# Two gate pairs by seven products instead of one, 18 filler blocks instead of 20, and tiles of their own for the scan's x, in a hybrid attention and state-space block

## The chip, the cores and the metric

The kernel runs on one core of a Trainium2 chip. The metric is the device time of one execution in microseconds (us). Five engines work side by side and wait for one another by semaphores: PE (TensorE, matmuls), ACT (ScalarE), DVE (VectorE), POOL (GpSimd) and SP (SyncE), which here does nothing but issue DMA transfers, in the order of its queue.

## The reference, cut to what matters

One layer: a token mixer of three branches (multi-head latent attention, forgetting attention, Mamba-2 scan), each gated by a sigmoid, then a gated MLP. S = 1024 positions, width 1024.

```
hn = rms_norm(x, norm_mix_g)
u_mla, u_fox, u_ssm, u_gate = split(hn @ w_in)
y_a = mla_branch(u_mla) @ w_br_mla;  y_b = fox_branch(u_fox) @ w_br_fox
y_c = ssm_branch(u_ssm) @ w_br_ssm
g = sigmoid(u_gate + b_gate)                  # 3 x 1024 columns
x = x + (g0*y_a + g1*y_b + g2*y_c) @ w_out
x = x + conv_ffn(rms_norm(x, norm_ffn_g))

ssm_branch: z, xBC, dt = split(u_ssm); xBC = silu(causal_dwconv(xBC))
            xs, B, C = split(xBC); y = ssd_scan(xs*dt, ...) + xs*D
            return rms_norm(y * silu(z))
ssd_scan:   by chunks: y = (C B^T * decay) x  +  C h * exp(a);  h = h*decay + B^T (decay x)
```

The gates need 3 x 1024 columns of `hn @ w_in`: 24 blocks of 128 columns, called gate blocks here. Their only reader is the product with the branches, late in the kernel.

## The kernel before, in words

Each fp32 operand of a matmul is split into a high and a low part (`..h`, `..l`), and three products are made (high x high, high x low, low x high). The high part is an ACT copy (L134), the low part a DVE subtraction (L135, and L1400 for filler weights). A matmul is 128x128 by 128x512.

The kernel goes through stages. Times are from the start of the profiled span: projections and their norms (to 396 us), the **convolution phase** (396 to 541), the **attention** of 16 heads (541 to 877), the **scan** in 8 chunks of 128 positions (877 to 1079), the branch products with the gates (L2145), the output product, and the MLP.

**Convolution phase.** It works in units n = 0, 1, ... A unit makes two blocks of 128 columns at once with seven half-size products (`c_product`, 12 matmuls each, L1224: 84 matmuls) where two blocks made directly take 96. Units 0 to 5 make the 12 blocks of xBC, whose convolution (`conv`) is stored to `xbc_d` (L1238); each unit from 6 on makes one pair of gate blocks (`pair_gates`), stored to `g_d` (L1309). `GP` is the number of these pairs. For a unit the sums of weights are made on POOL (`conv_sums`) and split on ACT and DVE. At the end one more gate block, `gates[1]`, is made directly (L1321, 48 matmuls); its weights are `raw_b` (L1261).

**Filler.** The other gate blocks (`all_fill`, 48 matmuls each, L1428, tiles `mm`) are put between the matmuls of the attention and the scan, so that PE has work while these wait for other engines. A block's weights are loaded (`wr`, L1392), split (`wh`, `wl`), and its result passes through ACT's tanh to a tile of the ring `f_t4` (four tiles, tag `t4`) and to `g_d` (L1438). In the attention a planner, the class `Sim`, writes out the order of PE, ACT, DVE and POOL; its second argument is the microseconds of filler by its own costs that it may spread over the heads (10.4 for a block). What is left is `f_left`; `FILL_SSD` gives an eighth of (`f_left` - 29) to each step of the scan.

**Scan.** Chunk c goes through three generators: `ssd_a` (loads; the transposes of x, L1922, tiles `stp` of a ring of two PSUM banks; B's transposes and C B^T in a third use of that ring, L1933 and L1935; on DVE `xd` L1941, `xddl` L135, `bTl`, and `cbm` L1938, which reads the bank of L1935), `ssd_b` (state update L1964 and its DVE part, `hsl`) and `ssd_c` (outputs `py` L1990, norm, transposes of y). `merge` interleaves `ssd_a` of chunk c, `ssd_b` of c-1, `ssd_c` of c-2 and filler on PE by fixed costs; the other engines follow a scheduler's order. Since the ring `stp` has two banks, the first group of x transposes of chunk c+1 takes the bank that C B^T of chunk c stood in, and cannot start before `cbm` of chunk c has read it.

The x tile of a chunk (`load_xs`, L1908, from `xbc_d`) is taken from the ring `f_t4`, which the filler outputs and z tiles (L1969) use too; `ssd_a` of chunk c, after its own transposes of x, asks for that of chunk c+1.

Of the kernel before, what the change touches and what calls it, by code (L numbers as in the profile page):

```python
# [11 lines left out]
F32 = mybir.dt.float32  # L12
# [9 lines left out]
P = 128  # L22
D = 1024
S = 1024
NT = S // P
# [17 lines left out]
def block_kernel(ctx: ExitStack, tc: tile.TileContext, x, positions, norm_mix_g, w_in, b_gate,  # L43
# [7 lines left out]
    def TP(name, bufs, **kw):  # L51
        if kw.get("space") != DRAM:
            kw["reuse_waits"] = "tile"
        return tc.tile_pool(name=name, bufs=bufs, **kw)
# [72 lines left out]
    def uid(s):  # L127
        cnt[0] += 1
        return f"{s}_{cnt[0]}"
# [495 lines left out]
    with ExitStack() as pm:  # L625
# [165 lines left out]
        def fx_bank():  # L791
            return acc("fx", "mv" if units % 3 == 2 else "mm")
# [179 lines left out]
            yield  # L972

    gates = [(b, j) for b in (1, 0, 2) for j in range(NK)]
    GP = 1

    def gate_cols(b, j):
        return w_inv[:, :, C_G + b * D + j * P:C_G + b * D + j * P + P]
# [57 lines left out]
    with ExitStack() as px:  # L1036
# [70 lines left out]
        for n, (which, c0) in enumerate(chunks):  # L1107
# [11 lines left out]
            for t in range(NT):  # L1119
# [8 lines left out]
                p = fx_head[t] if units < 6 else fx_bank()  # L1128
# [30 lines left out]
        for half in range(2):  # L1159
            p = fx_bank()  # L1160
# [30 lines left out]
    with ExitStack() as pc_:  # L1191
# [24 lines left out]
        def c_bank():  # L1216
            return psp.tile([P, 512], F32, name=uid("cb"), tag="up", bufs=6)
# [34 lines left out]
        late = []  # L1252
        last_n = 5 + GP
        for n in range(last_n + 1):
# [61 lines left out]
        for half in range(2):  # L1316
            p = c_bank()
# [64 lines left out]
    f_t4 = Ring(fpl, [P, S], F32, "t4", 4)  # L1382
# [27 lines left out]
    def all_fill():  # L1410

        blocks = [(b, j, C_G + b * D + j * P) for b, j in gates[2 + 2 * GP:]]
        f_left[0] = 10.4 * len(blocks)
# [33 lines left out]
    fill = all_fill()  # L1447
# [57 lines left out]
    def load_head(pool, br, h):  # L1505
        o = Head()
        o.br, o.h = br, h
        if (8 * br + h) % 2 == 0:
            t = [e[:, i, :] for e in (w0p.tile([P, 2, S], F32R, name=uid(n), tag=n) for n in ("w0h", "w0l"))
                 for i in range(2)]  # L1510
        else:
            t = [pool.tile([P, S], F32R, name=uid(n), tag=n, bufs=1) for n in ("qk0", "qk1", "qk2", "qk3")]
        if br == 0:
            parts = ((0, 0, k_h), (1, 0, k_l), (2, 0, q_h), (3, 0, q_l))
            kh, kl, qh, ql = (e[0:96] for e in t)
            o.passes = ((t[2][0:104], t[0][0:104]), (qh, kl), (ql, kh))
        else:
            parts = ((0, 0, fk_h), (1, 0, fk_h[:, 0:64, :]), (1, 64, fk_l), (2, 0, fq_h), (2, 64, fq_h), (3, 0, fq_l))
            o.passes = ((t[2], t[1]), (t[3][0:68], t[0][0:68]))
        for i, r, src in parts:  # L1520
            n = src.shape[1]
            SY.dma_start(f32(t[i][r:r + n, :]), src[h])
        return o

    def load_values(pool, o):
        o.vv = pool.tile([P, NT, P], F32R, name=uid("vv"), tag="vv")
        SY.dma_start(f32(o.vv), (v_d, fv_d)[o.br].rearrange("(t p) h c -> p t h c", p=P)[:, :, o.h, :])
# [174 lines left out]
    with ExitStack() as pt__:  # L1702
# [144 lines left out]
        with tc.manual_schedule(engines={mybir.EngineType.PE, mybir.EngineType.Activation, mybir.EngineType.DVE,  # L1847
                                         mybir.EngineType.Pool}):
            work = 227.0
            sm = Sim(fill, 86, work, 2.0)  # L1850
            sim[0] = sm
            ends = {}

            def head(hd, at):
                heads[hd] = load_head(atp, *names[hd])
                load_values(atp, heads[hd])
                loaded_at[hd] = at

            def make(hd):
                for jp in range(4):  # L1860
                    rows_, v = unit_tasks(sm, hd, jp, 4 * hd + jp)
                    ends[hd] = (rows_[-1].last, v)
                if hd + 2 < 16:
                    s_, v_ = ends[hd]
                    sm.add(Task("D", (0.3, 0.3), lambda hd=hd: head(hd + 2, sm.now.start + 8.0), [s_, v_], 0.0, (0, hd)))

            made = [0]

            def more(q=None):
                if made[0] < 16 and made[0] in heads:  # L1870
                    make(made[0])
                    made[0] += 1

            head(0, 1.0)
            head(1, 6.0)
            more()
            more()
            sm.run(more)
            clk[0] = max(sm.free.values())
            sim[0] = None  # L1880
# [8 lines left out]
    frp = pfr.enter_context(TP("frp", 1, side="right"))  # L1889
    with ExitStack() as ps__:  # L1890
# [12 lines left out]
            SY.dma_start(o.bc, xbc_d[8:12, :, c * P:c * P + P].rearrange("j p s -> p j s"))  # L1903

        def load_xs(o, c):
            o.xs, _ = f_t4.get()
            o.xs = o.xs.rearrange("p (j s) -> p j s", j=8)
            SY.dma_start(o.xs, xbc_d[0:8, :, c * P:c * P + P].rearrange("j p s -> p j s"))  # L1908

        def hb(t, c, hs=slice(0, 16)):  # L1910
# [2 lines left out]
        def ssd_a(o, c):  # L1913

            if c + 1 < NT:
                load_bc(obj[c + 1], c + 1)
                load_rows(obj[c + 1], c + 1)
            xT = pool.tile([P, D], F32, name=uid("xT"), tag="xT", bufs=1)
            for g in range(2):
                pt = psp.tile([P, 512], F32, name=uid("stp"), tag="tp", bufs=2)  # L1920
                for j in range(4):
                    T.transpose(pt[:, j * P:j * P + P], o.xs[:, 4 * g + j, :], ident)  # L1922
                A.activation(xT[:, 512 * g:512 * g + 512], pt, AF.Copy)
                yield 0.44
            yield 0.0
            if c + 1 < NT:
                load_xs(obj[c + 1], c + 1)
            o.bT = [pool.tile([P, 2, P], F32R, name=uid(n), tag=n) for n in ("bTh", "bTl")]
            o.c_ = [pool.tile([P, 2, P], F32R, name=uid(n), tag=n) for n in ("Ch", "Cl")]
            cbm = pool.tile([P, 2, P], F32, name=uid("cbm"), tag="cbm")  # L1930
            pt = psp.tile([P, 4, P], F32, name=uid("stp"), tag="tp", bufs=2)
            for g in range(2):
                T.transpose(pt[:, g, :], o.bc[:, g, :], ident)  # L1933
            for g in range(2):
                T.matmul(pt[:, 2 + g, :], o.bc[:, g, :], o.bc[:, 2 + g, :], start=True, stop=True)  # L1935
            split(*o.bT, pt[:, 0:2, :])
            split(*o.c_, o.bc[:, 2:4, :])
            V.tensor_mul(cbm, pt[:, 2:4, :], tri.unsqueeze(1).to_broadcast([P, 2, P]))  # L1938
            xv = xT.rearrange("p (h d) -> p h d", d=64)
            o.xd = pool.tile([P, 16, 64], F32, name=uid("xd"), tag="xd")  # L1940
            V.tensor_mul(o.xd, xv, hb(dt, c))  # L1941
            o.xdd = [pool.tile([P, 16, 64], F32R, name=uid(n), tag=n, bufs=1) for n in ("xddh", "xddl")]
            xdd = pool.tile([P, 16, 64], F32, name=uid("xdd"), tag="xdd", bufs=1)
            if c + 1 < NT:
                G.tensor_mul(xdd, xv, hb(dend, c))
            o.y = pool.tile([P, 16, 64], F32, name=uid("y"), tag="y", bufs=3)
            G.tensor_mul(o.y, xv, Db.unsqueeze(2).to_broadcast([P, 16, 64]))
            yield 0.65
            o.E = []
            for q in range(4):  # L1950
                E = pool.tile([P, 4, P], F32, name=uid("E"), tag="E", bufs=4)
                for hh in range(4):
                    h = 4 * q + hh
                    A.activation(E[:, hh, :], o.row[:, h, :], AF.Relu, scale=-1.0, bias=cumc[:, c, h:h + 1])
                A.activation(E, E, AF.Exp, scale=-1.0)
                V.tensor_mul(E, E, cbm[:, q // 2:q // 2 + 1, :].to_broadcast([P, 4, P]))
                o.E.append(E)
                if q == 1 and c + 1 < NT:
                    split(*o.xdd, xdd)
                yield 0.0  # L1960
# [71 lines left out]
        with tc.manual_schedule(engines={mybir.EngineType.PE}):  # L2032
            obj = {c: Head() for c in range(NT)}
            load_bc(obj[0], 0)
            load_xs(obj[0], 0)
            load_rows(obj[0], 0)
            merge([], 6.0)
            grain[0] = 4
            for c in range(NT + 2):
                st = []  # L2040
                if c < NT:
                    st.append((ssd_a(obj[c], c), 1.6))
                if 0 <= c - 2 < NT:
                    st.append((ssd_c(obj[c - 2], c - 2), *((0.88, 0.6) if c <= NT else (8.0, 0.2))))
                if 0 <= c - 1 < NT:
                    st.append((ssd_b(obj[c - 1], c - 1, obj.get(c - 2)), 6.4, 0.05))
                merge(st, FILL_SSD[c])
            for _ in range(4):
                if advance(fill) is None:
                    break  # L2050
# [234 lines left out]
    for t, nh in units:  # L2285
# [20 lines left out]
        p = head[t] if early else psp.tile([P, 512], F32, name=uid("wo"), tag="up", bufs=6)  # L2306
# [323 lines left out]
```

## Time and profile before

| | |
|---|---|
| median of three runs | 1989.72 us (1987.88, 1989.72, 1990.76) |
| profiled execution | 1986.64 us, its span 1984.9 us, mean granted clock 0.998 |
| convolution phase, in the span | 396.42 to 540.58 us |
| attention | 540.58 to 877.50 us |
| scan | 877.50 to 1079.15 us |
| matmuls of L1224 / L1321 / L1428 | 588 / 48 / 960 |

The profile lists how long each engine was busy; the chain of work that ended last, followed back from the end; and, for any stretch, busy times and single instructions with the idle time before them in square brackets and what released them. Matmul ends are modelled: matmuls that run back to back overlap in these records, so a matmul's price is the distance between starts. The 12 matmuls of a product or of a filler piece are grouped as x12 in the chain.

### The profile page before, as it was taken

Reading aid. Unit: us, or ns where it says so; the run is one execution under the profiler, and the core shown is the slowest. Engines: PE = TensorE matmul, PEld = TensorE weight load, DVE = VectorE, ACT = ScalarE, POOL = GpSimd, SP = SyncE. Lnnn points to the kernel's source line nnn. Section 1 sums busy time; section 2 is a strip of 40 time slices with the busy share of each in tenths; the row PEclk is TensorE's granted clock in tenths of the full one; section 3 lists DMA queues with packets and bytes.
Section 4 is the critical chain, followed back from the end, with each engine's and each line's share of the span. In section 5 each row is a group of like instructions: output and inputs, shape, how many; then the busy total and the mean of one; then the engine's idle time right before and its main releaser. Section 6 shows DMA issues by size and latency. Waiting matters only on the chain.

```text
span 1984.9 us, 28475 instructions
## 1 busy us (share of the span) xinstructions
PE 1958.7 (99%) x10101; PEld 1668.1 (84%) x10101; DVE 1397.4 (70%) x2156; ACT 965.8 (49%) x1678; POOL 701.3 (35%) x666
## 2 busy tenths in 40 slices
PE   9999999999999999998999999999999999999999
PEld 8989888888899988887888888888878888888887
DVE  7777567879566766757884575558997777766555
ACT  5555322355466666766774232225554444544432
POOL 5133232056123222213340351101664444423655
PEclk9999999999999999999999999999999999999999
DMA  6166856333645556545665785333323211249575
GB/s 180 53 197 212 269 189 211 103 106 112 197 123 145 134 144 149 145 127 172 179 193 172 260 289 190 124 121 107 106 85 96 75 53 54 85 157 333 194 260 191
DMA packets 278409, 312.18 MB, mean 157 GB/s; under 512 B 19213, under 2 KB 209305, under 8 KB 278266
## 3 DMA queue, kind: packets, MB, share of 16 engines
q1 hardware_dynamic: 278264, 310.35, 50.5%
q8 instruction: 80, 1.31, 0.3%
q14 instruction: 63, 0.52, 0.1%
q10 hardware_dynamic: 2, 0.00, 0.0%
HBM read 217.17 MB, written 93.13 MB: 156 GB/s over the span
## 4 chain that ended last, share of the span: by engine, by line
PE 88%; DVE 4%; issue 3%; DMA 2%; ACT 2%; POOL 1%; SPq 0%; DVEq 0%; ACTq 0%; POOLq 0%
PE mm L1428 10%; PE dn L2577 10%; PE ybr L2145 9%; PE fx L798 7%; PE cb L1224 7%; PE ua L2236 6%; PE uc L2236 5%; PE ud L2236 5%; PE wo L2281 4%; PE s L1737 4%; PE tp L1804 3%; PE ub L2236 2%; PE fxv L188 2%; PE py L1990 1%; PE o L1824 1%
## 5 line engine op out<-in xcount | busy, mean ns | idle before, releaser
L1764 POOL TENSOR_SCALAR pm<-pm,rs 128x128 f32<-128x128 f32 (+7 forms) x128 | 95.2, 748 | 249.7 <-DVE rs L1762 217.3
L2577 PE MATMUL dn<-dr,dr 128*128 128x512 f32 x592 | 182.3, 389 | 0.0
L1428 PE MATMUL mm<-hnh,wh 128*128 128x512 f32 x320 | 133.1, 416 | 0.9 <-DVE o L1788 0.9
L2577 PEld LDWEIGHTS dn<-dr,dr 128*128 128x128 f32 x592 | 111.1, 188 | 22.9
L1428 PE MATMUL mm<-hnh,wl 128*128 128x512 f32 x320 | 126.4, 395 | 0.0
L1428 PE MATMUL mm<-hnl,wh 128*128 128x512 f32 x320 | 126.3, 395 | 0.0
L1756 ACT ACTIVATE pm<-s,nmx 128x128 f32<-128x128 f32 (+7 forms) x128 | 94.8, 741 | 64.6 <-DVE nmx L1751 56.3
L2577 PE MATMUL dn<-dr 128*128 128x512 f32 x296 | 115.3, 390 | 0.0
L1812 DVE TENSOR_TENSOR ptl<-tp,pth 128x512 fp32r<-128x512 f32 (+1 forms) x160 | 96.7, 631 | 24.5 <-ACT pth L1808 22.6
L135 DVE TENSOR_TENSOR dr<-dr,dr 128x1024 fp32r<-128x1024 f32 x52 | 73.0, 1413 | 51.2 <-ACT dr L134 41.8
L135 DVE TENSOR_TENSOR wl<-S,wh 128x1024 fp32r<-128x1024 f32 x55 | 82.9, 1507 | 34.8 <-ACT wh L134 34.8
L1751 DVE TENSOR_REDUCE nmx<-s 128x1 f32<-128x128 f32 (+7 forms) x128 | 93.5, 747 | 11.9 <-PE s L1737 7.4
L2145 PE MATMUL ybr<-al,wh 128*128 128x512 f32 x256 | 99.8, 390 | 0.0
L2145 PE MATMUL ybr<-ah,wl 128*128 128x512 f32 x256 | 99.8, 390 | 0.0
L2145 PE MATMUL ybr<-ah,wh 128*128 128x512 f32 x256 | 99.7, 389 | 0.0
L1808 ACT ACTIVATE pth<-tp 128x512 fp32r<-128x512 f32 (+1 forms) x160 | 82.6, 552 | 20.6 <-PE tp L1804 18.7
L134 ACT ACTIVATE wh<-wr 128x1024 fp32r<-128x1024 f32 (+1 forms) x47 | 42.4, 902 | 100.5 <-PE ybr L2145 39.5
L134 ACT ACTIVATE wh<-S 128x1024 fp32r<-128x1024 f32 x55 | 58.3, 1059 | 65.1 <-PE uc L2236 47.1
L134 ACT ACTIVATE dr<-dr 128x1024 fp32r<-128x1024 f32 x52 | 55.0, 1061 | 71.5 <-PE dn L2577 49.8
L1804 PE MATMUL tp<-ident,pm 128*128 128x128 f32 x576 | 81.1, 272 | 0.0
L135 DVE TENSOR_TENSOR wl<-wr,wh 128x1024 fp32r<-128x1024 f32 (+1 forms) x47 | 55.1, 1172 | 36.3 <-ACT wh L134 36.2
L2454 DVE SCALAR_TENSOR_TENSOR fa<-cg,pc_f,fa 128x1023 f32<-128x1023 f32 (+1 forms) x44 | 74.3, 1688 | 1.4 <-ACT fa L2449 1.4
(612 smaller groups left out, 6220.2 us busy)
## 6 DMA issues: line engine op xcount, KB each, us to landing
dr<-act_d SPq DMA_DIRECT2D x99, 256.0 KB
wr<-in_w_in_dram SPq DMA_DIRECT2D x35, 512.0 KB
gl<-g_d SPq DMA_DIRECT2D x24, 512.0 KB
wr<-in_ffn_w_up_dram SPq DMA_DIRECT2D x23, 512.0 KB
ws<-in_ffn_w_down_dram SPq DMA_DIRECT2D x22, 512.0 KB
wsum_d<-ws SPq DMA_DIRECT2D x22, 512.0 KB
act_d<-fa SPq DMA_DIRECT2D x22, 512.0 KB
g_d<-t SPq DMA_DIRECT2D x20, 512.0 KB
```

The lines of the kernel that those rows point to most:

```text
L134: i = A.activation(h, src, AF.Copy) if he is A else he.tensor_copy(h, src)
L135: return i, le.tensor_sub(l, src, f32(h))
L798: T.matmul(p, a(k), b(k), start=k == 0 and i == 0, stop=k == NK - 1 and i == 2)
L1224: T.matmul(ps, a, b, start=first and i == 0, stop=i == 11, skip_group_check=not first)
L1428: T.matmul(ps, a[:, k, :], b[half][:, k, :], start=(k == 0 and i == 0), stop=(k == NK - 1 and i == 2))
L1756: A.activation(r.p[:, 0:cols], r.row, AF.Exp, bias=r.nmx[:, 0:1], accum_out=r.rs[:, 0:1])
L1764: r.norm = Task("G", (d - 0.025, d), lambda: G.tensor_scalar(r.p[:, 0:cols], r.p[:, 0:cols], r.rs[:, 1:2], 0.0, op0=ALU.mult, op1=ALU.add) ...
L1804: T.transpose(x.pt[:, c * P:c * P + P], rows_[qi].p[:, k * P:k * P + P], ident)
L1812: V.tensor_sub(x.tl[:, :off], x.pt[:, :off], f32(x.th[:, :off]))
L2145: T.matmul(pss[half], w_[:, k, :], a_[k][:, hs], start=k == 0 and i == 0, stop=k == nk - 1 and i == 2)
L2236: T.matmul(ps, a, b, start=first and n == 0, stop=n == 11, skip_group_check=not first)
L2577: T.matmul(ps[m], a[:, ts_], b[:, 512:], start=first_ and j == 0 and q == 0, stop=j == NFH - 1 and q == 2, skip_group_check=not first_)
```

## The change

`GP` goes from 1 to 2: the convolution phase gets unit 7 (a second pair of gate blocks), and the filler begins two blocks later, with 18 blocks. The planner's filler budget in the attention goes from 86 to 66. `load_xs` takes its tile from the pool `frp`, tags `ws0` and `ws1` by the parity of the chunk, instead of the ring; chunks 0 and 1 are loaded ahead of the scan, and `ssd_a` of chunk c asks for chunk c+2 after its own transposes. `frp`'s tags are otherwise first used after the scan. The lines after 2035 move by one.

```diff
@@ -972,7 +972,7 @@
     gates = [(b, j) for b in (1, 0, 2) for j in range(NK)]
-    GP = 1
+    GP = 2
@@ -1847,7 +1847,7 @@
             work = 227.0
-            sm = Sim(fill, 86, work, 2.0)
+            sm = Sim(fill, 66, work, 2.0)
@@ -1903,8 +1903,8 @@
         def load_xs(o, c):
-            o.xs, _ = f_t4.get()
-            o.xs = o.xs.rearrange("p (j s) -> p j s", j=8)
+            o.xs = frp.tile([P, 2, 512], F32, name=uid("xs"), tag=f"ws{c % 2}").rearrange(
+                "p a s -> p (a s)").rearrange("p (j s) -> p j s", j=8)
             SY.dma_start(o.xs, xbc_d[0:8, :, c * P:c * P + P].rearrange("j p s -> p j s"))
@@ -1923,8 +1923,8 @@
             yield 0.0
-            if c + 1 < NT:
-                load_xs(obj[c + 1], c + 1)
+            if c + 2 < NT:
+                load_xs(obj[c + 2], c + 2)
@@ -2032,7 +2032,8 @@
             load_bc(obj[0], 0)
-            load_xs(obj[0], 0)
+            for c in range(2):
+                load_xs(obj[c], c)
             load_rows(obj[0], 0)
```

By the orders of the two kernels L1224 has 672 matmuls instead of 588 and L1428 864 instead of 960. Of these 864, 384 stand in the attention (432 before), 30 between it and the scan's first transposes (30 before), and 450 behind those (498 before). From C B^T of one chunk to that of the next, for chunks 0 to 6, the filler matmuls were 36, 48, 48, 48, 60, 48, 48 and are 36, 48, 36, 48, 48, 36, 48; the last 12 of the 48 lie ahead of C B^T of chunk 0.

SP's queue where the convolution phase ends. Before: two stores of xBC, the weights of a filler block, a store, the weights of the next, a store, and the loads of head 0's q and k.

```order
L1261 DMA wr_5667<-in_w_in_dram 128x8x128
L1238 DMA xbc_d<-ca_5474 128x1024
L1238 DMA xbc_d<-ca_5609 128x1024
L1392 DMA wr_5904<-in_w_in_dram 128x8x128
L1238 DMA xbc_d<-ca_5616 128x1024
L1392 DMA wr_5910<-in_w_in_dram 128x8x128
L1238 DMA xbc_d<-ca_5750 128x1024
L1522 DMA w0l_5887<-q_h 104x1024
L1522 DMA w0h_5886<-k_h 104x1024
```

After, the same place; `xs` are the new x tiles of chunks 0 and 1.

```order
L1261 DMA wr_5813<-in_w_in_dram 128x8x128
L1238 DMA xbc_d<-ca_5616 128x1024
L1392 DMA wr_6036<-in_w_in_dram 128x8x128
L1238 DMA xbc_d<-ca_5751 128x1024
L1238 DMA xbc_d<-ca_5758 128x1024
L1309 DMA g_d_83<-cg_5693 128x1024
L1309 DMA g_d_83<-cv_5803 128x1024
L1522 DMA w0l_6019<-q_h 104x1024
L1522 DMA w0h_6018<-k_h 104x1024
L1522 DMA w0h_6018<-k_l 96x1024
L1522 DMA w0l_6019<-q_l 96x1024
L1392 DMA wr_6042<-in_w_in_dram 128x8x128
```

The first filler weights now share a two-tile tag with `raw_b` and come two transfers behind it; two gate stores stand ahead of head 0's loads; directly behind the last row shown come the loads of x for chunks 0 and 1.

PE's queue at C B^T of chunk 0 (L1935; `t_2355` is the x tile of chunk 1). Before:

```order
L1428 MATMUL mm_10670<-hnh_118,wl_10590 128x512
L1933 MATMUL stp_10704<-ident,bc_10580 128x128 x2
L1935 MATMUL stp_10704<-bc_10580 128x128 x2
L1922 MATMUL stp_10759<-ident,t_2355_10697 128x128 x4
L1428 MATMUL mm_10765<-hnh_119,wh_10589 128x512
```

After (12 matmuls of filler, of which the first two and the last one are shown apart):

```order
L1933 MATMUL stp_10764<-ident,bc_10652 128x128 x2
L1935 MATMUL stp_10764<-bc_10652 128x128 x2
L1428 MATMUL mm_10744<-hnh_118,wh_10663 128x512
L1428 MATMUL mm_10744<-hnl_120,wh_10663 128x512
...
L1428 MATMUL mm_10744<-hnh_118,wl_10664 128x512
L1922 MATMUL stp_10833<-ident,xs_10656 128x128 x4
L1428 MATMUL mm_10839<-hnh_119,wh_10663 128x512
```

The first x transposes of chunk 1 stood directly behind C B^T of chunk 0; 12 filler matmuls stand between them now.

DVE's queue from `xddl` to `cbm` of chunk 2. Before:

```order
L135 TENSOR_TENSOR xddl_11075<-xdd_11076,xddh_11074 128x1024
L135 TENSOR_TENSOR Cl_11282<-bc_10946,Ch_11281 128x256
L2001 TENSOR_TENSOR yo_11045<-pof_11041,ea 128x512
L135 TENSOR_TENSOR hsl_11081<-hst_10973,hsh_11080 128x1024
L2002 TENSOR_TENSOR y_10877<-y_10877,yo_11045 128x512
L1400 TENSOR_TENSOR wl_11019<-wr_11016,wh_11018 128x1024
L135 TENSOR_TENSOR bTl_11058<-stp_11062,bTh_11057 128x256
L1938 TENSOR_TENSOR cbm_11061<-stp_11062,tri 128x256
```

After (left out: seven rows, four of the state update, `xd`, and one each of `y` and `yo`):

```order
L1400 TENSOR_TENSOR wl_10937<-wr_10934,wh_10936 128x1024
...
L135 TENSOR_TENSOR xddl_11124<-xdd_11125,xddh_11123 128x1024
L2002 TENSOR_TENSOR y_10932<-y_10932,yo_11080 128x512
L135 TENSOR_TENSOR Cl_11323<-bc_11005,Ch_11322 128x256
L2001 TENSOR_TENSOR yo_11087<-pof_11083,ea 128x512
L135 TENSOR_TENSOR hsl_11136<-hst_11034,hsh_11135 128x1024
L2002 TENSOR_TENSOR y_10932<-y_10932,yo_11087 128x512
L135 TENSOR_TENSOR bTl_11107<-stp_11111,bTh_11106 128x256
L1938 TENSOR_TENSOR cbm_11110<-stp_11111,tri 128x256
```

Filler's low part (L1400) stood between `xddl` and `bTl`; it stands eight rows ahead of `xddl` now, and from `xddl` to `cbm` come only the scan's own steps.

## The prediction

> **What bounds the kernel.** I read the page first: the span, the busy line, the chain by engine.
>
> ```profile
> span 1984.9 us, 28475 instructions
> PE 1958.7 (99%) x10101; PEld 1668.1 (84%) x10101; DVE 1397.4 (70%) x2156; ACT 965.8 (49%) x1678; POOL 701.3 (35%) x666
> PE 88%; DVE 4%; issue 3%; DMA 2%; ACT 2%; POOL 1%; SPq 0%; DVEq 0%; ACTq 0%; POOLq 0%
> ```
>
> PE is the bound, 99% busy by the modelled ends. So a matmul taken away gains where PE never waits; where matmuls cover waits, it may gain nothing. The stages say which is where (columns: length, then busy time of PE, its weight loads, DVE, ACT, POOL, then the granted clock, DMA share, GB/s):
>
> ```profile
> 396.42:540.58 144.16, 144.16 (x638) 119.39 (x637) 108.95 (x87) 73.10 (x88) 69.16 (x38) 1.00 0.45 133
> 540.58:877.50 336.92, 336.00 (x2257) 299.57 (x2255) 233.28 (x488) 226.67 (x508) 95.17 (x128) 1.00 0.52 134
> 877.50:1079.15 201.65, 191.75 (x1045) 163.80 (x1045) 138.04 (x185) 134.16 (x281) 60.39 (x79) 0.98 0.57 178
> 895.96:1042.04 146.08, 137.10 (x765) 117.78 (x764) 116.95 (x154) 103.40 (x220) 54.51 (x63) 0.98 0.58 180
> ```
>
> The convolution phase has no PE idle time and DVE at 76%; the attention almost none; the scan 9.9 us, of which 9.0 lie in the fourth window, from C B^T of chunk 0 to that of chunk 7. What these idle times are, the chain and PE's timeline show:
>
> ```profile
> 396.42 133.28 PE cb L1224 x588
> 529.70 10.88 PE cb L1321 x48
> 893.92 6.37 DMA t<-xbc_d
> 901.06 4.34 PE mm L1428 x12
> 906.79 2.75 PE mm L1428 x12
> 939.35 3.95 issue
> 943.30 1.09 PE stp L1922 x4
> 944.39 3.59 PE mm L1428 x12
> ```
> ```profile
> 896.18 0.61 PE L1935 MATMUL stp<-bc 128*128 128x128 f32 x4
> 900.43 0.63 PE L1922 MATMUL stp<-ident,t 128*128 128x128 f32 x4 [3.64 <-DMA t<-xbc_d]
> 927.67 0.61 PE L1922 MATMUL stp<-ident,t 128*128 128x128 f32 x4
> 943.30 1.09 PE L1922 MATMUL stp<-ident,t 128*128 128x128 f32 x4 [3.96 <-issue]
> 965.83 0.63 PE L1922 MATMUL stp<-ident,t 128*128 128x128 f32 x4 [1.38 <-issue]
> ```
>
> Three waits, 3.64 + 3.96 + 1.38 = 8.98 us: the x tile of chunk 1 came late from memory, and the first x transposes of chunks 3 and 4 waited for their bank.
>
> **The products.** Unit 7 adds 84 matmuls at 133.28/588 = 0.2267 us: +19.04, all on the path, since PE never waits there. It also brings work for the others: by a seventh of the phase's, DVE 15.6, ACT 10.4, POOL 9.9 beside 19.04 of PE, so PE stays the bound. The filler loses 96 matmuls. At the same 0.2267 (L1321: 10.88/48) that is -21.76 if PE is the bound wherever they stood. Net **-2.72**.
>
> **x tiles of their own.** The load of chunk 1's x went out at 893.92 behind the store of a filler result in SP's queue and took 6.37 us; PE stood for 3.64. Chunk 1's load now stands in the queue behind head 0's loads, hundreds of us ahead, and later chunks' loads go out one step (18 to 25 us) ahead of use: the wait is gone. Behind it the 12 filler matmuls took 4.34 instead of 2.75, 1.59 more, which goes too: **-5.2** (between 0, if another wait ends the same stretch, and -5.23). Even without the new tiles, 12 filler matmuls (2.7 us) now stand ahead of these transposes.
>
> **The bank's wait.** The chain calls it "issue", but in code the transposes of chunk c+1 wait until `cbm` of chunk c has read the bank. DVE's timeline for chunks 2 and 3:
>
> ```profile
> 932.35 1.23 DVE L1941 TENSOR_TENSOR xd<-xT,dt 128x1024 f32<-128x1024 f32 x1 [2.52 <-ACT xT L1923]
> ...
> 936.47 2.27 DVE L135 TENSOR_TENSOR xddl<-xdd,xddh 128x1024 fp32r<-128x1024 f32 x1 [0.58 <-ACT xddh L134]
> ...
> 939.59 1.21 DVE L135 TENSOR_TENSOR hsl<-hst,hsh 128x1024 fp32r<-128x1024 f32 x1
> ...
> 941.32 1.21 DVE L1400 TENSOR_TENSOR wl<-wr,wh 128x1024 fp32r<-128x1024 f32 x1
> ...
> 942.79 0.41 DVE L1938 TENSOR_TENSOR cbm<-stp,tri 128x256 f32<-128x256 f32 x1
> ```
> ```profile
> 965.32 0.41 DVE L1938 TENSOR_TENSOR cbm<-stp,tri 128x256 f32<-128x256 f32 x1
> ```
>
> `cbm` ended at 943.20 and PE went on at 943.30; at 965.73, and PE at 965.83. From the end of the x transposes of chunk 2 (927.67 + 0.61) to `cbm`'s end are 14.9 us. For chunk 3, whose second group started at 952.78, it was 12.3:
>
> ```profile
> 952.78 0.61 PE L1922 MATMUL stp<-ident,t 128*128 128x128 f32 x4
> ```
>
> What PE has to do between the second x transposes of c and the first of c+1 has to cover this. From 928.28 to 939.35, where PE ran out, it had 11.1 us of work, 24 filler matmuls among it. By the orders the scan's own work there stays much the same and the filler matmuls differ, in pieces of 12 at 2.75: before, 24 in chunks 2 and 3 and 36 in chunks 4, 5 and 6; now 24 in chunks 3, 4 and 6 and 36 in chunks 2 and 5. So the cover is about 11.3 us or 14.0. So the two places that waited, after chunks 2 and 3, become one (3), and two new ones (4 and 6) come. In their favour the filler's low part (1.21) no longer stands ahead of `cbm`. I take 12.5 for the latency and so 1.2 at each of three places, 3.6 us. Before it was 3.96 + 1.38, and behind 943.30 the transposes took 1.09 instead of 0.6 and the 12 matmuls 3.59 instead of 2.72: 6.7 in all. **-3.1**, between -6.7 (no wait left) and +20 (below).
>
> **The attention with 48 fewer filler matmuls.** Their own time is in the first term. What they covered may come up. The chain of the attention by lines:
>
> ```profile
> by line: PE mm L1428 29.2%; PE s L1737 25.5%; PE tp L1804 17.6%; PE o L1824 6.3%; PE o L1816 6.0%; PE o L1819 3.4%; PE o L1818 3.3%; PE s L1741 1.4%; PE o L1823 1.1%; PE o L1822 1.1%; PE o L1821 1.0%; issue 1.0%; ACT pm L1756 0.7%; DVE nmx
> ```
>
> PE's entries add to 95.9%; 4.1% of 336.5 us, 13.8, is other work, in many pieces. The filler there was 432 x 0.2267 = 97.9 and becomes 87.1. If the uncovered part grows as the cover shrinks, 13.8 x (97.9/87.1 - 1) = 1.7; I take **+2**, between 0 and 10.9 (all 48 gain nothing). The planner spreads the rest by its own costs, and DVE stands at 233.28/336.92 = 69%, so I stay near the low end.
>
> **SP's queue where the attention begins.** The first filler weights wait for `raw_b` to be split, and the queue stands behind them, with head 0's loads. Before:
>
> ```profile
> 504.97 0.38 SPq L1392 DMA_DIRECT2D wr<-in_w_in_dram  x1
> ...
> 518.63 0.33 SPq L1522 DMA_DIRECT2D w0l<-q_h  x1
> 519.06 0.35 SPq L1522 DMA_DIRECT2D w0h<-k_h  x1
> ...
> 519.85 0.42 SPq L1522 DMA_DIRECT2D w0l<-q_l  x1
> ```
> ```profile
> 519.73 1.23 DVE L135 TENSOR_TENSOR wl<-wr,wh 128x1024 fp32r<-128x1024 f32 x1 [0.63 <-ACT wh L134]
> 540.58 2.72 PE mm L1428 x12
> ```
>
> That split ended at 520.96, so 19.04 later at about 540. Filler starts at 559.6 and the first scores behind it; loads of this size landed in 6.37 us (above). 0, covered by some 13 us of PE's work.
>
> **The sum.** -2.72 - 5.2 - 3.1 + 2 = -9.0. The profiled execution took 1986.64, so 1977.6; it lay 3.08 below the median of the runs, 1989.72, on which the change gives 1980.7. A change of less than 0.2%, 4 us, can't be told from none here. The most that the terms allow is -2.72 - 5.2 - 6.7 = -14.6, 1975.1.
>
> **Rivals.**
> *The scan gives back what its shorter steps gain (about no change).* Between 895.96 and 1042.04 PE's waits and slowed matmuls are 5.2 + 6.7 = 11.9; without them, and less 36 filler matmuls (8.2), 126.0 remain. DVE's 116.95, less about 0.9 for the filler's splits (1.21 for 48 matmuls), would be 92% of that. So a small delay on DVE goes straight to `cbm`. For it speaks that DVE's prices swing with its neighbours:
>
> ```profile
> L135 DVE TENSOR_TENSOR xddl<-xdd,xddh 128x1024 fp32r<-128x1024 f32 x7 | 14.7, 2102 | 2.6 <-ACT xddh L134 2.5
> L135 DVE TENSOR_TENSOR hsl<-hst,hsh 128x1024 fp32r<-128x1024 f32 x7 | 8.5, 1212 | 1.1 <-ACT hsh L134 1.1
> ```
>
> The same subtraction of the same shape takes 2102 or 1212 ns. One more such 0.9 us for each of seven chunks is 6.3: -2.7, so 1984 on the profile's base and 1987.0 on the median's. Against it: in the step from chunk 4's C B^T, with 14.0 of cover, nothing waited with DVE at 84% (18.45 of 22.04):
>
> ```profile
> 979.91:1001.95 22.04, 22.04 (x125) 18.90 (x123) 18.45 (x26) 17.55 (x36) 9.65 (x12) 1.00 0.67 203
> ```
>
> The Trainium skill, page "SBUF — State Buffer", section "Who interferes with whom", has a rule for the dear subtraction: a DVE instruction with two inputs in SBUF and a GpSimd instruction that reads SBUF exclude each other for a whole instruction, and who issues first goes first. The trace agrees as far as it goes: `xddl` runs where POOL has `y<-xT,Db` (2.35 us from 935.30). By that rule, which DVE rows are dear depends on where POOL's fall in shorter steps, and it would give the 1987.0 worked out above; by the rows of before alone, the latency stays near 12.5 and 1980.7 stands.
>
> *Slower.* DVE's latency is not 12.5 but chunk 2's 14.9 in each step, so that each of the five steps from chunk 2 to 6 waits like the one at 939.35: 3.96 plus 1.35 of slowed matmuls, 5.3. That is 26.5 instead of 6.7: -2.72 - 5.2 + 2 + 19.8 = +13.9, 2003.6. It decides once the scan's waits for the bank exceed 16.6, 3.3 a step. Chunk 2's 14.9 had a cause of its own: DVE waited 2.52 for ACT's copy of x, which ACT made late. The others had 12.3 to 13.7.
>
> *All of the bank's waits vanish,* because `cbm` comes sooner without the filler's low part: -14.6, 1975.1.
>
> That the change doesn't do what it says is out: matmuls and queues are in the order.
>
> **Chances.** The forecast 0.50 (between 1977 and 1985.5); all waits gone 0.14; the scan gives it back 0.24; slower 0.12. So faster 0.64, same 0.24, slower 0.12. The likeliest gives 1980.7; the range, 1974.5 to 1992, holds the first three and leaves out most of the slower case and the lowest of the fast one.
>
> **What would show it.** L1224 at 152.3 us with PE never idle; the attention's start 19 later and its length 326 to 330 (336.92 - 10.9 + 2 = 328); chunk 1's transposes without a wait for `xbc_d`; waits of 1 to 2 us in front of the first x transposes of chunks 4, 5 and 7; the stretch from C B^T of chunk 0 to chunk 7 at about 130 us. A wait of 3 us or more at every step, or an attention above 333, makes it wrong.

## The result: slower by 0.46%, and the profile after

The changed kernel takes 1998.78 us in the median of six runs (1995.38 to 2002.57), the kernel before 1989.66 in its six; the ratio is 1.0046, with the interval 1.0036 to 1.0056. The forecast was 1980.7, faster. The profiled executions of the changed kernel (2002.57) and, below, of pool_order (1992.16) and xs_only (1987.42) are the slowest of their runs, 3 to 5 us above their medians, and the stages shown are those of these executions.

The page, its span, busy line and chain by engine:

```profile
span 2000.8 us, 28472 instructions
PE 1964.8 (98%) x10089; PEld 1671.8 (84%) x10089; DVE 1402.7 (70%) x2161; ACT 969.1 (48%) x1682; POOL 720.2 (36%) x672
PE 79%; DVE 6%; DMA 4%; issue 4%; ACT 3%; POOL 3%; SPq 1%; ACTq 0%; DVEq 0%; POOLq 0%
```

PE's part of the chain fell from 88% to 79%: other engines hold it up. Where, the stages tell: the convolution phase, the attention, and C B^T of chunk 0 to that of chunk 7 (columns as in the prediction; these windows begin and end with a first matmul's start).

```profile
396.35:559.55 163.20, 163.20 (x721) 135.13 (x720) 117.95 (x94) 80.19 (x97) 80.08 (x44) 1.00 0.44 134
559.55:892.31 332.76, 328.00 (x2210) 291.09 (x2208) 231.53 (x488) 225.52 (x507) 96.32 (x128) 1.00 0.51 133
907.26:1056.41 149.15, 134.61 (x730) 116.08 (x729) 111.08 (x155) 105.31 (x223) 62.23 (x63) 0.92 0.54 170
```

Between the same matmuls before:

```profile
540.42:878.50 338.08, 336.25 (x2257) 299.73 (x2255) 233.70 (x489) 227.69 (x510) 95.17 (x128) 1.00 0.52 134
896.18:1042.26 146.08, 137.10 (x766) 117.78 (x765) 116.95 (x155) 103.62 (x220) 54.29 (x63) 0.98 0.58 179
```

The convolution phase grew by 19.04, as reckoned. The attention gave 5.3 back, not 8.9. The scan, with 36 filler matmuls fewer (8.2 us), should have shrunk and grew by 3.1, at a granted clock of 0.92 instead of 0.98. DVE, which the prediction watched, is less busy there than before. PE's waits in the scan, by what ended them (us in total, times, longest):

```profile
PE stp L2025 <- ACT y L2017: 11.2, 2, 7.3
PE pst L1964 <- DVE xddl L135: 3.0, 1, 3.0
```

The wait for `xbc_d` is gone and the one at the bank's transposes too. The new ones stand at the transposes of y (L2025) and at the first state update:

```profile
917.11 0.79 PE L1964 MATMUL pst<-xddl,bTh 128*128 128x512 f32 x1 [3.02 <-DVE xddl L135]
```
```profile
969.53 1.11 PE L2025 MATMUL stp<-ident,y 128*128 128x128 f32 x4 [7.32 <-ACT y L2017]
```
```profile
1016.13 1.11 PE L2025 MATMUL stp<-ident,y 128*128 128x128 f32 x4 [3.88 <-ACT y L2017]
```

L2017 scales y by the norm, whose reciprocal root is a chain of tiny steps on POOL (L2014, L176, then L179 and L180 three times). POOL's timeline of the changed kernel for chunk 1's norm:

```profile
955.75 0.78 POOL L2014 TENSOR_SCALAR yv<-yss 128x1 f32<-128x1 f32 x1 [11.31 <-ACT ysq L2012]
956.61 0.52 POOL L176 TENSOR_SCALAR rg_v<-yv 128x1 f32<-128x1 f32 x1
958.11 0.64 POOL L179 TENSOR_SCALAR rg_t<-yr,rg_v 128x1 f32<-128x1 f32 x1 [0.98 <-DVE yr L174]
958.71 2.87 POOL L1945 TENSOR_TENSOR xdd<-xT,dend 128x1024 f32<-128x1024 f32 x1
961.54 1.90 POOL L1947 TENSOR_TENSOR y<-xT,Db 128x1024 f32<-128x1024 f32 x1
963.44 1.74 POOL L180 TENSOR_SCALAR yr<-rg_t,yr 128x1 f32<-128x1 f32 x1
965.27 0.40 POOL L179 TENSOR_SCALAR rg_t<-yr,rg_v 128x1 f32<-128x1 f32 x1
965.77 0.27 POOL L180 TENSOR_SCALAR yr<-rg_t,yr 128x1 f32<-128x1 f32 x1
966.14 1.79 POOL L179 TENSOR_SCALAR rg_t<-yr,rg_v 128x1 f32<-128x1 f32 x1
968.03 0.27 POOL L180 TENSOR_SCALAR yr<-rg_t,yr 128x1 f32<-128x1 f32 x1
```
```profile
968.33 1.15 ACT L2017 ACTIVATE y<-y,yr 128x1024 f32<-128x1024 f32 x1 [2.72 <-POOL yr L180]
```

The same norm before:

```profile
951.03 0.34 POOL L179 TENSOR_SCALAR rg_t<-yr,rg_v 128x1 f32<-128x1 f32 x1 [2.55 <-DVE yr L174]
951.48 0.27 POOL L180 TENSOR_SCALAR yr<-rg_t,yr 128x1 f32<-128x1 f32 x1
951.84 0.34 POOL L179 TENSOR_SCALAR rg_t<-yr,rg_v 128x1 f32<-128x1 f32 x1
...
953.09 0.26 POOL L180 TENSOR_SCALAR yr<-rg_t,yr 128x1 f32<-128x1 f32 x1
954.82 1.91 POOL L1945 TENSOR_TENSOR xdd<-xT,dend 128x1024 f32<-128x1024 f32 x1 [1.47 <-ACT xT L1923]
```

Before, the three rounds take 2.3 us (951.03 to 953.35) and the two big products of chunk 3 come behind them. Now these products, 958.71 to 963.44, stand behind the first L179, and the rounds end at 968.30, 10.2 us after they began. ACT's L2017 starts at 968.33 and PE's transposes at 969.53: 7.32 us of PE. It happens again to chunk 3's norm, where the products of chunk 5 stand in the third round. In POOL's queue of the kernel before, no norm is broken. Nothing in the diff touches these lines. PE's order in the scan was written anew with less filler, and the order that the scheduler gives POOL went with it.

### The profile page after: what moved, and what is told of

The parts are those of the page before. It is cut to its first block, busy times and chain, and to the rows that moved or that the text cites. A ratio compares the mean times of both kernels' runs of the same rounds, so it can differ in the third digit from the quotient of the medians.

```text
span 2000.8 us, 28472 instructions
## 1 busy us (share of the span) xinstructions
PE 1964.8 (98%) x10089; PEld 1671.8 (84%) x10089; DVE 1402.7 (70%) x2161; ACT 969.1 (48%) x1682; POOL 720.2 (36%) x672
## 4 chain that ended last, share of the span: by engine, by line
PE 79%; DVE 6%; DMA 4%; issue 4%; ACT 3%; POOL 3%; SPq 1%; ACTq 0%; DVEq 0%; POOLq 0%
PE dn L2578 8%; PE cb L1224 8%; PE mm L1428 7%; PE ybr L2146 7%; PE fx L798 7%; PE ua L2237 6%; PE uc L2237 5%; PE ud L2237 4%; PE wo L2282 4%; PE s L1737 4%; PE tp L1804 2%; PE ub L2237 2%; PE fxv L188 2%; PE py L1990 1%; PE ckv L517 1%
## 5 line engine op out<-in xcount | busy, mean ns | idle before, releaser
L1428 PE MATMUL mm<-hnh,wh 128*128 128x512 f32 x288 | 121.3, 421 | 1.3 <-DVE o L1788 0.9
L1428 PE MATMUL mm<-hnh,wl 128*128 128x512 f32 x288 | 113.9, 395 | 0.0
L1428 PE MATMUL mm<-hnl,wh 128*128 128x512 f32 x288 | 113.7, 395 | 0.0
```

Of the source, the lines that this page charges most:

```text
L1428: T.matmul(ps, a[:, k, :], b[half][:, k, :], start=(k == 0 and i == 0), stop=(k == NK - 1 and i == 2))
```

## The experiments

Theory A: the loss in the scan is POOL's order. Theory B: the shorter steps have no room, and any order of POOL would give such a wait.

**pool_order.** In the changed kernel, `xdd` and y's product are kept behind what was written before them on POOL.

```diff
-                G.tensor_mul(xdd, xv, hb(dend, c))
+                tc.keep_in_program_order(G.tensor_mul(xdd, xv, hb(dend, c)))
-            G.tensor_mul(o.y, xv, Db.unsqueeze(2).to_broadcast([P, 16, 64]))
+            tc.keep_in_program_order(G.tensor_mul(o.y, xv, Db.unsqueeze(2).to_broadcast([P, 16, 64])))
```

> The changed kernel with the two POOL products of a chunk (xdd, L1945, and y<-xT,Db, L1947) kept behind the norm's steps that were written before them; the orders of PE and SP stay as they are. Theory A (the scan's loss is POOL's order: in chunks 3 and 6 these two products, 4.8 us, stand in the middle of the norm's chain of the chunk two before, and PE's transposes of y wait for it, 7.3 and 3.9 us): these two waits and the slowed matmuls behind them go, 8 to 14 us less than the changed kernel's 1998.8, so 1985 to 1991. Theory B (the scan has no room: the steps are short of cover whatever POOL's order is, and another wait, of the bank or of xddl, comes in their place): at most 4 us less, 1995 or more.

(The second broken norm is that of chunk 3, by the products of chunk 5; the text named chunk 6.) Measured: 1987.13 (1983.19 to 1992.16), 0.9985 of the kernel before (0.9975 to 0.9995), and 11.65 below the changed kernel, whose fastest run is slower than the slowest here. PE's waits in the scan:

```profile
PE pst L1964 <- DVE xddl L135: 3.4, 1, 3.4
PE stp L1922 <- issue: 2.2, 1, 2.2
PE stp L2025 <- ACT yT L2026: 1.3, 1, 1.3
...
PE stp L2025 <- ACT y L2017: 0.6, 1, 0.6
```
```profile
906.71:1047.06 140.35, 132.25 (x730) 113.33 (x729) 113.99 (x156) 105.17 (x224) 59.66 (x63) 0.95 0.56 182
```

The three rounds of chunk 1's norm run from 957.94 to 961.40 here, 3.5 us instead of 10.2. The 11.2 us of waiting for y are 0.6; 2.2 come back at the bank, and 1.3 are spent on ACT's copy of transposes of y (L2026). The stretch from C B^T of chunk 0 to that of chunk 7 is 8.8 us shorter. Theory A holds. The scheduler also moved some rows of DVE and ACT with POOL's products (`xddl` of chunks 3, 5 and 6 among them), so the 11.65 us belong to POOL's order together with what follows from it; the next run comes from the other side.

**broken_before.** The same cause put into the kernel before, with PE's order, filler, pair and tiles as they were: the second step of two norms is queued behind the products of a later chunk.

```diff
-            G.tensor_scalar(y, t, 1.5, y, op0=ALU.add, op1=ALU.mult)
+            step_[0].append(G.tensor_scalar(y, t, 1.5, y, op0=ALU.add, op1=ALU.mult))
...
-            G.tensor_mul(o.y, xv, Db.unsqueeze(2).to_broadcast([P, 16, 64]))
+            y_ = G.tensor_mul(o.y, xv, Db.unsqueeze(2).to_broadcast([P, 16, 64])); c in (3, 6) and behind_(obj[c - 2].steps[0], y_)
```

> The kernel before with one thing added: on POOL the norm's chain of chunks 1 and 4 stands behind the two products (xdd, y<-xT,Db) of chunks 3 and 6 from its first step on, as in the changed kernel. PE's order is that of before; filler, pair and x tiles too. Theory A (POOL's order makes the loss): 8 to 12 us more, 1998 to 2002, with PE waiting for ACT's scaled y (L2017) at the transposes of y. Rival (the breaks only hurt in the changed kernel's shorter steps, longer steps hide them): 0 to 3 more, 1990 to 1993.

(It breaks the norms of chunks 1 and 4, not 1 and 3.) Measured: 2005.78 (2004.75 to 2007.61), ratio 1.0084 (1.0070 to 1.0098): 16.6 us more, above the 8 to 12 that were expected. POOL at the norm of chunk 1:

```profile
950.58 0.34 POOL L179 TENSOR_SCALAR rg_t<-yr,rg_v 128x1 f32<-128x1 f32 x1 [3.50 <-DVE yr L174]
954.36 1.91 POOL L1945 TENSOR_TENSOR xdd<-xT,dend 128x1024 f32<-128x1024 f32 x1 [3.44 <-ACT xT L1923]
956.23 2.88 POOL L1947 TENSOR_TENSOR y<-xT,Db 128x1024 f32<-128x1024 f32 x1
959.11 1.74 POOL L180 TENSOR_SCALAR yr<-rg_t,yr 128x1 f32<-128x1 f32 x1
```

The cause is of the same kind and not of the same size: here POOL also stood idle inside the norm, 3.44 us at chunk 1 and 2.05 at chunk 4, until ACT had copied x for the product. PE's waits keep the two long ones of before and add the new ones:

```profile
PE stp L2025 <- ACT y L2017: 12.3, 2, 7.3
PE stp L1922 <- issue: 4.0, 1, 4.0
PE stp L1922 <- DMA t<-xbc_d: 3.5, 1, 3.5
```

The rest of the 16.6 goes with slowed matmuls behind the long waits (the granted clock from C B^T of chunk 0 to that of chunk 7 is 0.92, and was 0.98) and 2 us in the branch products; it was not taken apart further.

**pair_only and xs_only** take the change apart: the pair, 18 blocks and budget 66 with x tiles from the ring; and the new x tiles alone.

```diff
-    GP = 1
+    GP = 2
-            sm = Sim(fill, 86, work, 2.0)
+            sm = Sim(fill, 66, work, 2.0)
```
```diff
-            o.xs, _ = f_t4.get()
-            o.xs = o.xs.rearrange("p (j s) -> p j s", j=8)
+            o.xs = frp.tile([P, 2, 512], F32, name=uid("xs"), tag=f"ws{c % 2}").rearrange(
+                "p a s -> p (a s)").rearrange("p (j s) -> p j s", j=8)
...
```

> The second pair, 18 blocks and the budget 66, but the x tiles from the ring as before the change. PE's and POOL's orders are those of the changed kernel. If the x tiles have no part in the loss and 12 filler matmuls ahead of chunk 1's transposes cover most of the load's lateness: 1998 to 2003. If the early loads of x are what disturbs (SP's queue, the transfers of the rows beside them): 1990 or less.

> The x tiles of their own alone, with one pair, 20 blocks and the budget 86. PE's and POOL's orders are those of the kernel before. If the wait for x was a loss of its own, 4 to 5.2 us less than before: 1984.5 to 1986. If another wait ends the same stretch (the state update behind it waits for xddl, as it did after the change for 3.0 us): 0 to 2 less, 1988 to 1990.

pair_only: 1998.42 (1.0041, 1.0029 to 1.0054), the time of the whole change. xs_only: 1984.05 (0.9971, 0.9960 to 0.9982), 5.7 less than before. So the x tiles gain about what they promised where they are alone, and nothing beside the pair. (In xs_only's profile the stretch between the C B^T is only 2.0 shorter than before, 144.08; where the rest of the 5.7 lies, that profile does not show.) pair_only's waits say why:

```profile
PE stp L2025 <- ACT y L2017: 11.2, 2, 7.3
PE pst L1964 <- DVE xddl L135: 3.1, 1, 3.1
```

No wait for `xbc_d` is left even with the ring: the 12 filler matmuls that now stand ahead of chunk 1's transposes cover it. The stretch ends behind `xddl` of chunk 0 all the same.

**pool_order_b86, three_pairs, b96_first_x_pair** move filler in or out: `Sim(fill, 86, ...)` on pool_order; `GP = 3` on pool_order; and `Sim(fill, 96, ...)` on first_x_86 (below).

> As pool_order, and the planner's budget 86 in place of 66: 432 filler matmuls in the attention as before the change, 432 behind it (480 in the changed kernel). If filler covers more in the attention than in the scan (48 matmuls less there gained 5.4 of their 10.9 us): 2 to 5 us less than pool_order. If the scan's steps run out of cover with 36 to 48 instead of 36 to 48 with more 48s: the same or up to 6 us more.

> pool_order (1987.13) with a third pair, GP = 3, 16 blocks of filler, budget 66: 384 filler matmuls in the attention as there, 96 fewer in the scan. If a pair is worth its 12 matmuls wherever the filler stood: 2.7 less, 1984.4. If the scan's cover has run out (DVE alone is busy some 111 to 116 us between C B^T of chunks 0 and 7, and pool_order_b86 took 127.8 there): the 19 us of the pair come back by less than 19, 1988 to 1996.

> first_x_86 (1982.9, two pairs) with budget 96: 456 filler matmuls in the attention, 24 fewer in the scan. If the scan stands at its floor near 125 to 128 us (first_x_86 took 125.2): 5.4 more in the attention and nothing back, 1987 to 1989. If the scan still gives back what filler leaves it: 1982 to 1984.

Medians: 1985.65 (0.9977, 0.9968 to 0.9987), 2001.44 (1.0049, 1.0036 to 1.0062), 1987.47 (0.9994, 0.9985 to 1.0003). pool_order_b86 is 1.5 below pool_order, which is not clear of the noise and meets neither expectation; three_pairs is above both of its own; b96_first_x_pair is where a floor of the scan put it. The stages, as distances between first matmuls in each profiled execution, with the filler matmuls of the attention and behind it:

| kernel | filler, attention / behind | convolution phase | attention | C B^T 0 to 7 |
|---|---|---|---|---|
| before | 432 / 528 | 144.16 | 338.08 | 146.08 |
| changed | 384 / 480 | 163.20 | 332.76 | 149.15 |
| pool_order | 384 / 480 | 163.20 | 332.82 | 140.35 |
| pool_order_b86 | 432 / 432 | 163.20 | 338.37 | 127.81 |
| first_x_86 | 432 / 432 | 163.20 | 338.38 | 125.18 |
| b96_first_x_pair | 456 / 408 | 163.20 | 343.51 | 124.63 |
| three_pairs | 384 / 384 | 182.24 | 333.58 | 127.89 |
| xs_only | 432 / 528 | 144.16 | 338.16 | 144.08 |
| xs_b106 | 504 / 456 | 144.16 | 355.26 | 128.40 |

In the attention, 48 matmuls between 384 and 432 cost 5.3 to 5.6 of their 10.9 us; the 24 and 72 above 432 cost 5.1 and 17.1, all of their time (5.4, 16.3). In the scan, 432 or 384 or 408 behind the attention give 125 to 128 us: in these runs a matmul taken away from there on gains nothing. three_pairs pays 19.04 for its third pair; the scan, though 12.5 shorter than in pool_order's profile, is no shorter than pool_order_b86's with 48 more; and the median is 14.3 above pool_order's. At this floor DVE is busy nine tenths of the time; that DVE sets it was not tested:

```profile
911.88:1039.70 127.82, 117.42 (x683) 100.59 (x682) 115.20 (x154) 99.09 (x214) 57.33 (x63) 0.99 0.59 189
```

**first_x_86 and first_x_xs** ask why `xddl` of chunk 0 is late. ACT stands behind rows from memory that its products E (L1954) need, with 13 of the 16 ahead of its copy of chunk 0's x. Four now stand ahead.

```diff
-                    A.activation(E[:, hh, :], o.row[:, h, :], AF.Relu, scale=-1.0, bias=cumc[:, c, h:h + 1])
+                    (tc.keep_in_program_order if c == 0 else (lambda i: i))(A.activation(E[:, hh, :], o.row[:, h, :], AF.Relu, scale=-1.0, bias=cumc[:, c, h:h + 1]))
```

> As pool_order_b86 (1985.65), and for chunk 0 ACT's 16 products E (L1954), which wait for the rows from memory, are kept behind what was written ahead of them; in the order 4 of them, not 13, stand ahead of ACT's copy of chunk 0's x. Theory A (the wait for xddl of chunk 0, 2.7 to 3.4 us, took the place of the wait for x, because ACT copies x only behind E): most of that wait and the slowed matmuls behind it go, 2 to 4 us less, 1982 to 1984. Theory B (xddl is late because of DVE's own queue, or the rows are late for the 4 too): no change, 1985 to 1986.

> The same edit on xs_only (1984.05): one pair, 20 blocks, x tiles of their own. Its profile shows 1.1 us of wait for xddl. Theory A: 1 to 2.5 us less, 1981.5 to 1983. Theory B: 1984 within 1.

Measured: 1982.89 (0.9963, 0.9950 to 0.9975), against 1985.65 without the edit, and 1983.83 (0.9968, 0.9956 to 0.9980) against 1984.05. In the first the wait for `xddl`, 2.7 us, is gone from the list; in the second, where it had been 1.1, the gain is too small to be told. So ACT's order at the scan's start was the cause of that wait. What its going is worth is less sure: the intervals of the first pair overlap, and the waits at the bank and for y rose from 4.3 and 2.3 us to 5.7 and 3.4.

**xs_b106, b106_first_x_xs, b96_first_x_xs** keep one pair and 20 blocks, with the new x tiles, POOL's order kept, and the budget 106 or 96.

> xs_only (1984.05) with the planner's budget 106 in place of 86 and POOL's two products kept behind the norm: 504 filler matmuls in the attention instead of 432, 456 behind it instead of 528. In the attention 48 fewer matmuls gained 5.4 of 10.9 us; if 72 more cost half of their 16.3 there and save all of it in the scan: 4 to 8 less, 1976 to 1980. If the attention's waits are used up, or the scan's steps with 36 matmuls wait: 1984 or more.

> xs_b106 (1982.9) with chunk 0's E behind the copies of x. xs_b106 shows no wait for xddl. If that edit helps by that wait alone: no change, 1982 to 1984. If it also brings the scan's start forward: 1 to 2 less.

> One pair, x tiles of their own, POOL's products behind the norm, E of chunk 0 behind the copies of x, budget 96: 456 filler matmuls in the attention, 504 behind. By xs_b106's stages (the attention pays all that stands above 432; the scan saves while it is above some 128 us): 5.4 more in the attention than first_x_xs, 6 to 10 less in the scan: 1979 to 1983.

Measured: 1982.90 (0.9961, 0.9949 to 0.9974), 1981.47 (0.9967, 0.9956 to 0.9977), 1988.73 (0.9998, 0.9990 to 1.0007). xs_b106 came out above its 1976 to 1980, since the attention charged 17.1 for the 72 matmuls and not half; b106_first_x_xs is 1.4 below xs_b106, which is within the noise, so its two expectations are not parted; the last missed: its scan took 141.93, not the 133 to 137 that were reckoned, with 6.3 us of waits at the bank. The traces show where the difference lies: from C B^T of chunk 0 to that of chunk 7 stand 324 filler matmuls in xs_only, 312 in b96_first_x_xs and 288 in xs_b106, so of its 72 matmuls xs_b106 saves 36 there, 8.2 us. The other 7.5 us lie for the greater part in waits and slowed matmuls: xs_only waits 5.8 at the bank and 1.1 for `xddl` at a clock of 0.98, xs_b106 for neither, and 4.5 elsewhere, at 1.00. Why the waits at the bank go with one budget and stay with the other is open: each budget also gives the scan another order, and these runs do not part the two.

Against the runs of the kernel before beside each, the best are xs_b106, 7.5 us less, and first_x_86 and b106_first_x_xs, 7.5 and 7.7; they can't be told apart.

## Why the prediction was wrong, step by step

- *The products, -2.72.* The convolution phase went from 144.16 to 163.20, +19.04, PE never idle. Right. The 96 filler matmuls were priced at their full 21.76; in the attention 48 of them brought 5.3 of 10.9, and that is the fourth term.
- *x tiles, -5.2.* The step chose the high end, where its low end held: pair_only and the changed kernel take 1998.42 and 1998.78. The wait for x went by the 12 filler matmuls, as the prediction's last sentence on it allowed, with or without the tiles. "If another wait ends the same stretch" named the way, not the engine: `xddl` of chunk 0, 3.0 us, because ACT copies x late. Alone the tiles bring 5.7.
- *The bank's wait, -3.1.* The changed kernel shows no wait for `cbm`, but there PE had already stood for y; with POOL's order kept, one wait of 2.2 us is back at the bank, where the step had three of 1.2. So its size was about right and its places were not. But the step went through DVE's queue only, and the sum has no term for POOL. **This is where the prediction failed**: the transposes of y stand in the same queue of PE and wait for POOL's norm, and POOL's order of before and after was not laid side by side. It had changed in two places, where PE stood for 7.32 and 3.88 us with slow matmuls behind; keeping it brings 11.65 us (pool_order).
- *The attention, +2.* Right in kind, too small: +5.6 by the stage (-5.3 instead of -10.9).
- *SP's queue, 0.* Right: the convolution phase shows no wait, and the attention's start none for a load.
- *The sum.* Forecast -9.0, measured +9.1, 18.1 apart: POOL's order 11.65 and the attention 3.6 make 15.2; the other 3, by subtraction, are what the terms for x and the bank did not bring, and no run measures them by themselves.
- *The rivals.* The slower one had a chance of 0.12 and the wrong cause: a wait for the bank in each step, of which the changed kernel shows none. That its 2003.6 lies near the measured 1998.78 is luck. The rival that gave back the gain, by dearer subtractions on DVE, did not come either: `xddl` takes 1644 ns in the mean of the changed kernel's scan, and took 2102.
- *What would show it* listed chunk 1's transposes without their wait, which came, and waits at chunks 4, 5 and 7, which did not. The stretch that was to take about 130 us took 149.15, and the attention about 332 where 326 to 330 was forecast.

## What to carry to other kernels

Where one engine's order is written by hand and the others are left to a scheduler, compare the order of every engine, not only of those that waited before: here a chain of eight tiny steps cost PE nothing until two big products were queued into its middle. Put such a chain's neighbours behind it explicitly. And price filler by stage: in these runs a matmul of filler was worth its full time where nothing waited, and half of it or nothing where it covered a wait.

## What the runs showed of the hardware

A step of the norm of one element per partition takes 0.26 to 0.34 us on POOL in the rows of the kernel before shown above, where DVE has no instruction between 950.85 and 954.26. In the changed kernel two such steps, at 963.44 and 966.14, take 1.74 and 1.79, while DVE runs `xddl`, `hsl` and the additions L2002 behind them:

```profile
962.70 1.82 DVE L135 TENSOR_TENSOR xddl<-xdd,xddh 128x1024 fp32r<-128x1024 f32 x1 [0.46 <-ACT xddh L134]
964.44 0.68 DVE L2002 TENSOR_TENSOR y<-y,yo 128x512 f32<-128x512 f32 x1
...
965.98 1.21 DVE L135 TENSOR_TENSOR hsl<-hst,hsh 128x1024 fp32r<-128x1024 f32 x1
967.12 0.68 DVE L2002 TENSOR_TENSOR y<-y,yo 128x512 f32<-128x512 f32 x1
```

Each of the two POOL steps ends some 0.7 us after the DVE subtraction beside it (965.18 after 964.52, 967.93 after 967.19), and just behind the end of the addition (965.12 and 967.80). The Trainium skill, page "SBUF — State Buffer", section "Who interferes with whom", says that a DVE instruction with two inputs in SBUF contends with a POOL instruction that reads SBUF, for ports that only one of them holds at a time. The trace agrees as far as the ends of these rows go. Either side can pay: `hsl` takes its usual 1.21 us and the small step waits, but `xddl` takes 1.82 behind the product that POOL ends at 963.44. So a chain of small POOL steps that slips behind big ones can also meet DVE's subtractions, which come right after those.
